# Two-layer attention and retention trunk: background steps of the first group named round by round, and another order of the first supertile's list

## The chip, the core and the metric

The kernel runs on one core of a Trainium2 chip. The core has a matrix engine (TensorE, PE in the profile; its weight loads are PEld), a vector engine (VectorE, DVE), an activation engine (ScalarE, ACT), a general engine (GpSimd, POOL) and a queue that issues transfers (SyncE, SP). Each works through its own instructions in order and waits at the head of its queue for what the next instruction needs from another engine or a transfer. The metric is the device time of one execution in microseconds, the median over several runs.

## What is computed

Two layers over 2048 tokens of width 1024, float32 in and out, and a final RMS norm. The reference, cut to what matters:

```python
def hybrid_layer(x, norm_gain, w_in, w_out, rel_bias, cos, sin):
    hn = rms_norm(x, norm_gain)
    proj = hn @ w_in                       # 1024 x 4096
    aq, ak, av, ag, rq, rk, rv, rg = jnp.split(proj, cuts, axis=-1)
    ya = chunked_rel_attention(aq, ak, av, rel_bias)      # 8 heads x 64, own chunk + 8 before
    yr = chunkwise_retention(rq, rk, rv, cos, sin)        # 4 heads x 128, recurrent state
    y = jnp.concatenate([ya * silu(ag), yr * silu(rg)], axis=-1)
    return x + y @ w_out

def reference(x, positions, norm_gain, w_in, w_out, rel_bias, final_gain):
    cos, sin = rotary_tables(positions, RET_HEAD_DIM)
    for layer in range(DEPTH):
        x = hybrid_layer(x, norm_gain[layer], w_in[layer], w_out[layer], rel_bias[layer], cos, sin)
    return rms_norm(x, final_gain)
```

## The kernel before

**Precision.** Every large product is made of float16 halves: an operand is scaled by a power of two, its upper half is a float16 copy (ACT, the "hi" steps) and the remainder is a second float16 (DVE, the "lo" steps); three products of halves are added in PSUM. So normalised tokens are `hTh` and `hTl`, weights `wh` and `wl`.

**Tiling.** The tokens are 16 tiles of 128, four to a supertile of 512 (n = 0 to 3). The heads of a layer are four groups (s = 0 to 3) of two attention heads and one retention head. For each layer, group and supertile there is `dense_T` (L652), four outputs of 24 matmuls (q, k, rotary q and k, heads on the partitions), then `dense_V` (L784), four token tiles of 24 matmuls (v, retention v, gates), then `attention` (L823) with `retention` (L913). The attention of a supertile runs while the next supertile's dense work runs.

**Rounds.** `run` (L1222) walks through the dense generator. Eight dense matmuls are a round; `dense_T` and `dense_V` have 12 each. In each round, `run` first lets the dense generator issue its matmuls and, after 24, their eviction from PSUM; then `tick` issues small steps that were put off by a number of rounds with `later`; then one step of attention; then `pull` takes steps from background generators in `bg`, as many as needed to be done in time. All engines but SP take this written order. SP takes it up to the end of the first supertile (`sp_order`); after that the transfers are ordered by the framework, but for those under `in_turn`.

Attention issues the scores of a unit (token tile and head) every third round: matmuls (L845, L846), the bias and maximum on DVE (L849, L851), the exponential on ACT (L852), a float16 copy (L854), its remainder on POOL (L855), and a transposing transfer (L857). Retention's products (L902) need a masked score (DVE L921), its upper half (ACT L906) and the remainder (DVE L910), one round apart, and the same for the state `sh`.

**Before the first round.** The first supertile is ordered by hand in one list of step names, `do(...)` (L1433). Steps of token tile t: `xsq` square and sum (ACT), `xrs` root (a small DVE step L217 and a power on POOL L219), `xmul` product with the root and the gain (DVE), `xtr` transposes on PE, `xhi`, `xlo`, `xdma` transposing transfers on SP. Steps of weight section j, W for `dense_T` and V for `dense_V`: `sq` (ACT), `lp` a cast of the sum (DVE L1315), `sc` a sum over partitions on PE (L1321) and the scale (DVE L1328 to L1332), `hi`, `lo`. `g` computes the gain's scale, `t` and `u` are steps of the rotary tables 0, and 1 and 2, `r` reverses the relative bias, `bs` and `bt` spread it, `d` is a step of the first `dense_T`, `Tu` and `Vu` are small scale factors.

**Background in the first group (s = 0).** During `dense_V` of supertile 0 a generator of 12 rounds (L1438) finishes token tiles 4 to 7. During supertiles 1 and 2, `norms_from_input` (L1236) normalises token tiles 8 to 11 and 12 to 15, one after the other on a plan of 21 rounds, and the rotary tables run beside them; the sine is taken on ACT (L118, L119). During supertile 3, `prep_T` (L393) prepares the weights of `dense_T` of the next group; with its `dense_V` begins `prep_V` (L442), the weights of that group's `dense_V`. How many steps fall into one round is worked out by `run`.

**Shared buffers that the prediction names.** PSUM has two buffers for dense outputs, so an output waits until the one two before it was evicted by ACT and DVE (L677 and L680 for q, `qq`; L694 and L697 for k, `kk`; L805 to L815 for dense_V). The buffer of `qq` is also that of rk's `raw` in the first supertile, and `kk`, `swp` share one. `swp` receives the swapped halves by transfer (L715, L716), POOL rotates (L719 to L721), ACT and DVE split (L724, L727).

Of the kernel before, what the change touches and what calls it, by code (L numbers as in the profile page):

```python
# [8 lines left out]
F16 = mybir.dt.float16  # L9
# [4 lines left out]
ALU = mybir.AluOpType  # L14
# [4 lines left out]
P = 128  # L19
# [8 lines left out]
def hybrid_trunk(ctx: ExitStack, tc: tile.TileContext, x, pos, gain, gcol, w_in, w_out, rel, fgain,  # L28
# [364 lines left out]
    def prep_T(l, s, g, halves=False, w=None):  # L393
        w = w or Sections(l, s, g, halves)
        if (l, s) == (0, 1):
            w.load(0)
            w.load(1)
            for j in range(4):
                for _ in range((2, 2, 0, 1)[j]):
                    yield  # L400
                w.square(j)
                if j in (0, 2):
                    w.load((j + 4) // 2)
                yield
                if j:
                    w.scale(j - 1)
                    yield from w.split(j - 1)
            yield
            w.scale(3)
            yield from w.split(3)  # L410
            return
# [242 lines left out]
    def dense_T(l, s, n, g, st):  # L654
# [4 lines left out]
        def tab_load():  # L659
            while n not in tab_done:  # L660
                pull(1)
            in_turn(sp.dma_start(st.tabc, tab_d[n][0]))
            in_turn(sp.dma_start(st.tabs, tab_d[n][1]))
# [103 lines left out]
        for j in range(2 if first else 0, 4):  # L767
            if j == 2 and not first:
                tab_load()
            if first:  # L770
                ps = psR.tile([P, 512], F32, tag="small", name=f"dT{nm}_{j}")
            else:
                ps = psD.tile([P, 512], F32, tag="dense", name=f"dT{nm}_{j}")
            while g.tdone <= j:
                pull(1)
            m = 0
            for kt, (w_, h_) in in_order(j == 0, ((g.h, hh), (g.l, hh), (g.h, hl))):
                pe.matmul(ps, w_[:, j, kt, :], h_[:, kt, :], start=(m == 0), stop=(m == 23))  # L778
                m += 1
                if m in (8, 16) or (m == 24 and first):  # L780
                    yield
            evacuate(j, ps)
            yield

    def dense_V(l, s, n, g, st):
# [4 lines left out]
        st.rv, st.g = [], []  # L790
        while g.vdone < 4:
            pull(1)
        for a in range(4):
# [441 lines left out]

    def norms_from_input(ts, spaces, rows, tab):  # L1236

        def load(k):
            u = us[k]
# [4 lines left out]
        def sq(k):  # L1244
            u = us[k]
# [3 lines left out]
        def root(k):  # L1249
            us[k].rs = rms_of(us[k].ss, gains[0].m, gains[0].e, us[k].nm)  # L1250

        def mul(k):
            u = us[k]
            dve.scalar_tensor_tensor(out=u.x, in0=u.x, scalar=u.rs[:, 0:1], in1=gains[0].b, op0=ALU.mult, op1=ALU.mult)

        def hi(k):
            us[k].rows = rows[k % 2]
            rows_hi(us[k].rows, us[k].x)

        def lo(k):  # L1260
            rows_lo(us[k].rows, us[k].x)

        def dma(k):
            transpose_rows(us[k].rows, *us[k].h)

        us = []
        for t in ts:
            u = St()
            u.t, u.nm = t, f"n0_{t}"
            us.append(u)  # L1270
        plan = {0: [lambda: load(0)]}
        add = lambda r, fn, k: plan.setdefault(r, []).append(lambda: fn(k))
        for k in range(4):
            if k:
                add(4 * k - 4, load, k)
            for i, fn in enumerate((sq, root, mul, hi, lo, dma)):
                add(3 + 4 * k + i, fn, k)
        for r in range(21):
            for fn in plan.get(r, ()):
                fn()  # L1280
            next(tab, None)
            yield
        for _ in tab:
            yield

# [141 lines left out]

    def rounds(lists):
        for names in lists:
            do(names)  # L1430
            yield

    do("xsq0 g g xrs0 g Wsq0 Wlp0 Wsc0 xmul0 xtr0 Whi0 xsq1 xhi0 xrs1 xlo0 xmul1 Wlo0 xsq2 d t Wsq1 xrs2 xtr1 t xhi1 Wlp1 xmul2 "  # L1433
# [3 lines left out]
    g00.vdone = 4  # L1437
    push(rounds(["xhi4 xrs5 xrs6", "xlo4 xmul5 xrs7", "xdma4 xhi5 xmul6 bt", "xlo5 xhi6", "xdma5 xlo6 xmul7", "xdma6 xhi7",  # L1438
                 "xlo7", "xdma7 bt", "x8 u", "u x8 bt", "u u x8", "u u x8 bt"]), 12)
    att = [None]  # L1440
    for l in range(DEPTH):
        gO = [Grp(), Grp()]
        go = Grp()
        for s in range(NSW):
            g = grp(l, s)
            for n in range(NS):
# [12 lines left out]
                if (l, s) == (0, 0) and 0 < n < NS - 1:  # L1459
                    if n == 1:  # L1460
                        push(t1, TAB_STEPS - 7)
                    pairs = [xs0[0], w4.tile([P, D], F32, tag="w4", name="rows8") if n == 1 else xs0[1]]
                    pairs = [(w_[:, 0:D], w_[:, D:2 * D]) for w_ in (r_.bitcast(F16) for r_ in pairs)]
                    push(norms_from_input(range(4 * n + 4, 4 * n + 8), late[0:4] if n == 1 else None, pairs,
                                          iter(()) if n == 1 else tables((3,), [xs0[3][:, i * 256:(i + 1) * 256] for i in range(4)])), 21)
                if (l, s, n) == (0, 1, 1):
                    for l_ in range(1, DEPTH):
# [3 lines left out]
                        later(18, lambda gr=gr: next(gr))  # L1471
                if n == (NS - 1 if (l, s) == (0, 0) else 1):
                    if s + 1 < NSW:
                        push(prep_T(l, s + 1, grp(l, s + 1)), 25 if (l, s) != (0, 0) else 19)
                    else:
# [9 lines left out]
                if not first:  # L1485
                    run(dT, att, 12 if last else 10 if n == 0 else 18 if (l, s, n) == (0, 0, NS - 1) else 22 if (l, s) == (0, 0) else 24)
                if n == NS - 1:
                    if s + 1 < NSW:
# [94 lines left out]
```

## Time and profile before

| | us |
|---|---|
| median of 3 runs | 2059.97 (2055.54 to 2060.03) |
| the profiled execution | 2058.52 |
| its span, first to last instruction | 2056.7 |
| PE busy in the span | 1996.4 |
| DVE busy | 1239.1 |
| ACT busy | 1134.8 |
| POOL busy | 685.7 |

How to read it: an engine's busy time is the time in which it executes instructions, not waits. The mean clock granted to PE over the span is 0.993 of full speed. Matmuls are pipelined, so the duration of one (some 0.38 us for 512 columns) is longer than the distance between two starts. A row of waits names the waiting engine, its tile and line, the instruction that ended the wait, the total in us, how often, and the longest.

### The profile page before, as it was taken

To read this page: it belongs to the slowest core of one execution; us is meant where nothing else is said; L and a number is where in the kernel's file an instruction comes from. 1 tells how busy PE (TensorE), PEld (TensorE's weight loads), DVE (VectorE), ACT (ScalarE), POOL (GpSimd) and SP (SyncE) were. 2 spreads that over 40 slices of the span, in tenths; PEclk is the share of its full clock that TensorE was granted. 3 is DMA by queue.
4 is the path that set the end of the run, shared out by engine and by line. 5 is a ranking of instruction groups with operands and counts; after the bars stand their busy time and mean duration, and the time that the engine had idled before them with its cause. 6 is when DMAs were issued, how large, how long until landed. Compare 5 with 4: busy or idle time off the path is not lost. (4 is left out here: it accounts for less than half of the span.)

```text
span 2056.7 us, 36849 instructions
## 1 busy us (share of the span) xinstructions
PE 1996.4 (97%) x12918; PEld 1048.5 (51%) x12918; DVE 1239.1 (60%) x3676; ACT 1134.8 (55%) x2526; POOL 685.7 (33%) x701
## 2 busy tenths in 40 slices
PE   6998999999999999999999999999999999999998
PEld 4444554555555555554444555555555555555444
DVE  7676666566556655667553656565655566557543
ACT  7556665556565654655444546554656565455432
POOL 0243343444344433430003433443343434343100
PEclk9999999999999999999999999999999999999999
DMA  8677764557584754799874547454656765558874
GB/s 233 165 167 171 156 148 108 113 110 167 112 185 112 165 135 103 161 205 276 223 180 114 129 104 156 116 126 102 160 118 147 155 155 129 123 116 185 226 203 137
DMA packets 645690, 313.47 MB, mean 152 GB/s; under 512 B 459232, under 2 KB 602080, under 8 KB 645504
## 3 DMA queue, kind: packets, MB, share of 16 engines
q1 hardware_dynamic: 645504, 311.12, 64.8%
q8 instruction: 101, 1.65, 0.3%
q14 instruction: 85, 0.70, 0.1%
HBM read 123.26 MB, written 41.98 MB: 80 GB/s over the span
## 5 line engine op out<-in xcount | busy, mean ns | idle before, releaser
L855 POOL TENSOR_TENSOR pq<-sc,pq 128x640 f16<-128x640 f32 (+4 forms) x256 | 319.7, 1249 | 862.9 <-ACT pq L854 445.4
L852 ACT ACTIVATE sc<-sc,mq,cT 128x640 f32<-128x640 f32 (+4 forms) x256 | 218.4, 853 | 615.7 <-DVE mq L851 448.5
L797 PE MATMUL dV<-whV,hTh 128*128 128x512 f16 x1024 | 352.8, 380 | 4.8 <-DVE gt L815 4.6
L797 PE MATMUL dV<-whV,hTl 128*128 128x512 f16 x1024 | 352.8, 380 | 0.0
L797 PE MATMUL dV<-wlV,hTh 128*128 128x512 f16 x1024 | 352.5, 380 | 0.0
L778 PE MATMUL dT<-hTh,whT 128*128 128x512 f16 x1008 | 348.6, 381 | 3.7 <-DVE kk L697 1.3
L778 PE MATMUL dT<-hTl,whT 128*128 128x512 f16 x1008 | 347.2, 380 | 0.0
L778 PE MATMUL dT<-hTh,wlT 128*128 128x512 f16 x1008 | 347.2, 380 | 0.0
L797 PEld LDWEIGHTS <-hTh 128*128 128x128 f16 x2048 | 196.3, 98 | 221.4 <-DVE gt L815 7.0
L778 PEld LDWEIGHTS <-whT 128*128 128x128 f16 x2016 | 192.5, 98 | 209.9 <-issue 4.6
L849 DVE CUSTOM_DVE_ANT_0 sc<-S,bias 128x640 f32<-128x640 f32 (+4 forms) x256 | 188.4, 736 | 82.5 <-PE S L846 81.0
L1175 PE MATMUL dO<-whO,yhy 128*128 128x512 f16 x504 | 191.5, 380 | 1.5 <-DMA yhy<-hTh 1.5
L1175 PE MATMUL dO<-whO,yly 128*128 128x512 f16 x504 | 191.5, 380 | 0.5 <-DMA yly<-hTh 0.5
L1175 PE MATMUL dO<-wlO,yhy 128*128 128x512 f16 x504 | 191.7, 380 | 0.0
L854 ACT ACTIVATE pq<-sc 128x640 f16<-128x640 f32 (+4 forms) x256 | 171.5, 670 | 8.1
L1175 PEld LDWEIGHTS <-yhy 128*128 128x128 f16 x1008 | 98.3, 98 | 114.8 <-DMA yhy<-hTh 2.0
L797 PEld LDWEIGHTS <-hTl 128*128 128x128 f16 x1024 | 99.1, 98 | 111.9 <-issue 2.9
L778 PEld LDWEIGHTS <-wlT 128*128 128x128 f16 x1008 | 97.3, 98 | 114.7 <-issue 7.3
L845 PE MATMUL S<-k,q 128*128 128x128 f16 (+3 forms) x592 | 142.8, 268 | 0.0
L867 PE MATMUL o<-v,pT 128*128 128x129 f16 x1120 | 133.8, 222 | 5.4 <-DMA pT<-pq 5.4
L846 PE MATMUL S<-k,q 128*128 128x128 f16 (+3 forms) x592 | 129.7, 267 | 0.0
L868 PE MATMUL o<-v,pT 128*128 128x65 f16 x1120 | 126.8, 194 | 0.0
(359 smaller groups left out, 3246.1 us busy)
## 6 DMA issues: line engine op xcount, KB each, us to landing
q<-qq SPq DMA_DIRECT2D x128, 128.0 KB, 2.4
yyy<-y_d SPq DMA_DIRECT2D x32, 512.0 KB, 4.4
stT<-in_w_in_dram SPq DMA_DIRECT2D x27, 512.0 KB, 5.2
stV<-in_w_in_dram SPq DMA_DIRECT2D x26, 512.0 KB, 4.5
k<-kk SPq DMA_DIRECT2D x128, 64.0 KB, 2.0
swp<-rot SPq DMA_DIRECT2D x64, 128.0 KB, 3.1
tabc<-tab SPq DMA_DIRECT2D x32, 256.0 KB, 2.9
tabs<-tab SPq DMA_DIRECT2D x32, 256.0 KB, 3.1
```

What stands on the lines that cost most here:

```text
L778: pe.matmul(ps, w_[:, j, kt, :], h_[:, kt, :], start=(m == 0), stop=(m == 23))
L797: pe.matmul(ps, h_[:, kt, a * P:(a + 1) * P], w_[:, kt, :], start=(m == 0), stop=(m == 23))
L845: pe.matmul(o, st.q[:, hx, 0, cs], k_, start=True, stop=False)
L846: pe.matmul(o, st.q[:, hx, 1, cs], k_, start=False, stop=True)
L849: dve.tensor_tensor_reduce(out=v, in0=S[:, 0:w], in1=g.bias[hx][:, 640 - w:640], scale=1.0, scalar=-3.0e38, op0=ALU.add, op1=ALU.max, accu ...
L852: act.activation(v, v, AF.Exp, bias=m[:, 0:1], scale=g.c[:, 0:1])
L854: act.activation(pq[:, 0:w], v, AF.Copy)
L855: pool.tensor_tensor(pq[:, w:2 * w], v, pq[:, 0:w], op=ALU.subtract)
L867: pe.matmul(o[:, u.hx, 0:129], u.p[:, b, :], v_, start=(b == 0), stop=False)
L868: pe.matmul(o[:, u.hx, 0:65], u.p[:, u.nb + b, :], v_[:, 0:65], start=False, stop=(b == u.nb - 1))
L1175: pe.matmul(ps, h_[:, kt, :], w_[:, kt, :], start=(m == 0), stop=(m == 23))
```

## The change

The generators of the first group are replaced by named steps. `listed` has 96 entries, one for each round from `dense_V` of supertile 0 to the end of `dense_T` of the next group's supertile 0: rounds 0 to 11 are `dense_V` of supertile 0, 12 to 35 supertile 1, 36 to 59 supertile 2, 60 to 83 supertile 3, 84 to 95 that `dense_T`. An entry has two lists of names: the first is issued ahead of attention's step of the round, the second behind it. Later rounds have nothing listed, and `pull` works as before for the other groups.

```diff
@@ run
         for _ in gen:
             tick()
+            before, behind = next(listed, ("", ""))
+            do(before)
             if att[0] is not None and next(att[0], att) is att:
                 att[0] = None
             ring["att_done"] = att[0] is None
+            do(behind)
```

`norms_from_input` becomes `norm_steps`, which registers the same functions under names: `xin8` to `xin15` (the load; nothing is issued for 8 to 11, which `x8` loads), then `xsq`, `xrs`, `xmul`, `xhi`, `xlo`, `xdma`. `weight_steps` registers those of the next group's weights: `Tin`, `Tsq`, `Tsc`, `Thi`, `Tlo` for `dense_T` and `Uin`, `Usq`, `Usc`, `Uhi`, `Ulo`, `Uu` for `dense_V`, made from the same helpers as `prep_T` and `prep_V`; the special case for (0, 1) in `prep_T` goes.

```diff
+    def norm_steps(ts, spaces, rows):
...
+        for k, t in enumerate(ts):
+            u = St()
+            u.t, u.nm = t, f"n0_{t}"
+            for f, fn in (("in", load), ("sq", sq), ("rs", root), ("mul", mul), ("hi", hi), ("lo", lo), ("dma", dma)):
+                steps[f"x{f}{t}"] = lambda fn=fn, u=u, k=k: fn(u, k)
+
+    def weight_steps():
+
+        g = grp(0, 1)
+        w = Sections(0, 1, g)
...
+        def vsq(j):
+            m[j] = sumsq(sts[j], f"{nm}{j}", g.vh[:, :, j * P:(j + 1) * P])
+            if j == 3:
+                dve.tensor_tensor(m[2], m[2], m[3], op=ALU.add)
+            if j != 2:
+                m[j] = lowp(m[min(j, 2)], f"{nm}{j}")
+
+        def vsc(j):
+            sv, iv[j] = norm_scale(allsum(m[j if j < 2 else 3], f"{nm}{j}"), f"{nm}{j}", gains[0].i)
+            for i in ((j,) if j < 2 else (2, 3)):
+                vcv[i] = convert(sts[i], g.vh[:, :, i * P:(i + 1) * P], g.vl[:, :, i * P:(i + 1) * P], sv)
...
+        for j in range(4):
+            for f, fn in (("in", w.load), ("sq", w.square), ("sc", w.scale), ("hi", thi), ("lo", lambda j: drain(cv[j]))):
+                steps[f"T{f}{j}"] = lambda fn=fn, j=j: fn(j)
+            for f, fn in (("in", vload), ("sq", vsq), ("sc", vsc), ("hi", lambda j: next(vcv[j])), ("lo", vlo)):
+                steps[f"U{f}{j}"] = lambda fn=fn, j=j: fn(j)
+        steps["Uu"] = units
```

The lists themselves (`v` is a step of rotary table 3):

```diff
-    do("xsq0 g g xrs0 g Wsq0 Wlp0 Wsc0 xmul0 xtr0 Whi0 xsq1 xhi0 xrs1 xlo0 xmul1 Wlo0 xsq2 d t Wsq1 xrs2 xtr1 t xhi1 Wlp1 xmul2 "
-       "Wsc1 xsq3 Wsq2 xrs3 t xtr2 xlo1 xhi2 d Whi1 t xlo2 Wsq3 xmul3 d r Vsq0 Wlp2 Wlo1 t Wsc2 xtr3 Vsq1 r d xhi3 "
-       "t Vlp0 Whi2 Vsc0 t xlo3 Whi3 bs t d Vhi0 Wlo2 d Vhi1 Wlo3 t d d d Vlo0 t t Vsq2 d t Vlo1 t u Vsq3 t d Vlp2 t d t Tu Vsc2 t xsq4 "
-       "Vhi2 Vhi3 d d Vlo2 Vlo3 xsq5 d Vu d xsq6 xrs4 d Vu xmul4 xsq7 d")
+    do("xsq0 g g Wsq0 xrs0 Wlp0 xsq1 g Wsc0 t Whi0 xmul0 t xtr0 xrs1 Wlo0 xmul1 xsq2 xhi0 xrs2 Wsq1 xlo0 xtr1 xsq3 "
+       "Wlp1 xmul2 Wsc1 d xhi1 Whi1 xtr2 xrs3 xlo1 xhi2 t Wsq2 xlo2 Wsq3 xmul3 t Wlo1 d d Wlp2 Vsq1 r xtr3 t Vsq0 Wsc2 "
+       "d Vlp0 t xhi3 t Vsc0 Whi3 t xlo3 Vsq3 d Whi2 t r Vsq2 d Wlo2 t Vhi0 d d Wlo3 d bs Vlp2 d t Vlo0 d Vhi1 t xsq7 "
+       "t xsq4 d t Tu t xrs4 t t Vsc2 xmul4 xsq6 Vhi3 d Vhi2 u Vlo1 d Vlo2 d Vu xsq5 d Vlo3 Vu d d")
     g00.vdone = 4
-    push(rounds(["xhi4 xrs5 xrs6", "xlo4 xmul5 xrs7", "xdma4 xhi5 xmul6 bt", "xlo5 xhi6", "xdma5 xlo6 xmul7", "xdma6 xhi7",
-                 "xlo7", "xdma7 bt", "x8 u", "u x8 bt", "u u x8", "u u x8 bt"]), 12)
+    listed = iter([("bt xrs6 xhi4 xrs5", "xmul6 xlo4 xdma4"), ("xrs7 xmul5", ""), ("xhi5", "xmul7 xlo5"), ("", "xhi6 x8"),
+                   ("", "xdma5 u xlo6"), ("", "u xhi7"), ("xlo7 bt", ""), ("bt u", "u"), ("", ""), ("u u u", ""),
+                   ("", "xdma6 xdma7"), ("x8 u", "bt"), ("", "u x8"), ("u x8 xin11", ""), ("u", "u u u u"), ("", "u"),
+                   ("", "u"), ("", ""), ("", ""), ("xin9 xin8", ""), ("xsq8", "xrs8 xin10"), ("xsq9", "xmul8 xhi8 xrs9"),
+                   ("", "xmul9"), ("xhi9 xlo8", ""), ("xsq10", "xlo9"), ("xdma9", ""), ("xsq11 xdma8", "xrs10"),
+                   ("", "xrs11 xmul10"), ("xhi10", ""), ("", "xmul11 xlo10"), ("xhi11", "xlo11"), ("", "xdma10 xdma11"),
+                   ("", ""), ("", ""), ("", ""), ("", ""), ("xin12", ""), ("", "v"), ("xsq12", "xin13 v"), ("", "v"),
+                   ("xin14 v v", "xrs12 v"), ("xsq14 xmul12", ""), ("xhi12", "xlo12"), ("v v", "xsq13 xdma12"),
+                   ("v xrs13", "xrs14"), ("", "v"), ("xmul13", "xin15"), ("xhi13", ""), ("v", "v xlo13"),
+                   ("xmul14 v", ""), ("", "v xsq15"), ("xhi14 xrs15", "v"), ("xlo14 xdma13", "xmul15 xdma14"),
+                   ("", "v xhi15"), ("", ""), ("xlo15", ""), ("xdma15", ""), ("v", ""), ("v", ""), ("", ""),
+                   ("Tin0", "Tin1 Tsq1"), ("", ""), ("", "Tsq0"), ("", "Tin2"), ("", "Tsc1"), ("Tsc0 Tsq2", "Thi0"),
+                   ("", ""), ("Thi1 Tlo0", ""), ("", ""), ("", "Tsc2 Tlo1 Tin3"), ("", ""), ("Tsq3", ""),
+                   ("Thi2", "Tsc3"), ("", "Tlo2 Thi3 Tlo3"), ("", "Uin0"), ("Usq0", ""), ("", "Uin1"), ("", "Usc0 Uhi0"),
+                   ("", ""), ("Ulo0", ""), ("", ""), ("Usq1", ""), ("", ""), ("Usc1", "Uhi1"), ("", "Uin2 Ulo1"),
+                   ("", "Usq2"), ("Uin3", ""), ("Usq3", ""), ("", ""), ("", "Usc2 Uhi2"), ("", "Ulo2"), ("", ""),
+                   ("", "Uu Uhi3"), ("", ""), ("Ulo3", ""), ("", ""),])
```

Where the main loop pushed the generators for the first group it now registers steps:

```diff
-                    push(norms_from_input(range(4 * n + 4, 4 * n + 8), late[0:4] if n == 1 else None, pairs,
-                                          iter(()) if n == 1 else tables((3,), [xs0[3][:, i * 256:(i + 1) * 256] for i in range(4)])), 21)
+                    norm_steps(range(4 * n + 4, 4 * n + 8), late[0:4] if n == 1 else None, pairs)
+                    if n == 2:
+                        t3 = tables((3,), [xs0[3][:, i * 256:(i + 1) * 256] for i in range(4)])
+                        steps["v"] = lambda: go_on(t3)
...
-                if n == (NS - 1 if (l, s) == (0, 0) else 1):
+                if (l, s, n) == (0, 0, NS - 1):
+                    weight_steps()
+                elif n == 1 and (l, s) != (0, 0):
```

More of the change, by code (lines that the diff above doesn't have):

```diff
@@ L394, in prep_T @@
         w = w or Sections(l, s, g, halves)
[L395 to L411, printed above, removed]
         w.load(0)
@@ L1234, in run, with load @@
             left -= 1
-    def norms_from_input(ts, spaces, rows, tab):
-        def load(k):
-            u = us[k]
+    def norm_steps(ts, spaces, rows):
+        def load(u, k):
             u.x = spaces[k] if spaces else w4.tile([P, D], F32, tag="w4", name=f"xin{u.t}")
@@ L1254, in mul, with hi @@
+        def mul(u, k):
             dve.scalar_tensor_tensor(out=u.x, in0=u.x, scalar=u.rs[:, 0:1], in1=gains[0].b, op0=ALU.mult, op1=ALU.mult)
[L1256 to L1267, printed above, removed]
+        def hi(u, k):
+            u.rows = rows[k % 2]
+            rows_hi(u.rows, u.x)
@@ L1268, in norms_from_input, with lo, dma @@
+        def lo(u, k):
+            rows_lo(u.rows, u.x)
+        def dma(u, k):
+            transpose_rows(u.rows, *u.h)
+        for k, t in enumerate(ts):
             u = St()
             u.t, u.nm = t, f"n0_{t}"
[L1270 to L1277, printed above, removed]
```

49 lines of the change are left out of this document (28 added, 21 removed).

## The prediction

> **What bounds the kernel now.** I read the page's span and busy times first, then the waits of TensorE (PE), then the busy time of each engine by supertile, and last the queues of the other engines around the waits.
>
> ```profile
> span 2056.7 us, 36849 instructions
> PE 1996.4 (97%) x12918; PEld 1048.5 (51%) x12918; DVE 1239.1 (60%) x3676; ACT 1134.8 (55%) x2526; POOL 685.7 (33%) x701
> ```
>
> PE is the bound: 60.3 us of the span are without a matmul. No matmul is added or removed by the change, so it can win only PE's pauses and the time in which PE ran at a lower clock. Where those lie is seen by cutting the trace at the first dense matmul of each supertile. The columns are start:end, length, then busy us of PE, PEld, DVE, ACT and POOL, the granted clock, the DMA share and GB/s.
>
> ```profile
> 0.00:50.37 50.37, 33.31 (x298) 24.22 (x299) 35.82 (x105) 36.06 (x68) 4.88 (x18) 0.93 0.81 234
> 50.37:71.33 20.96, 20.89 (x97) 9.29 (x96) 17.12 (x29) 13.19 (x27) 6.51 (x8) 1.00 0.81 155
> ...
> 71.33:130.77 59.44, 51.51 (x278) 24.66 (x277) 42.30 (x96) 32.45 (x73) 23.48 (x26) 0.94 0.70 171
> 130.77:191.83 61.06, 54.30 (x363) 28.77 (x361) 43.73 (x116) 37.08 (x78) 24.30 (x23) 0.97 0.82 173
> 191.83:248.72 56.89, 54.14 (x369) 29.10 (x370) 34.94 (x118) 36.10 (x80) 20.97 (x19) 0.97 0.69 150
> 248.72:304.27 55.55, 52.57 (x366) 28.18 (x364) 33.26 (x111) 35.45 (x83) 21.53 (x23) 1.00 0.71 158
> ...
> 353.95:405.78 51.83, 51.83 (x363) 28.03 (x361) 31.74 (x99) 28.16 (x67) 21.43 (x20) 1.00 0.51 113
> 405.78:457.85 52.07, 52.07 (x370) 28.35 (x367) 31.26 (x92) 27.74 (x63) 20.14 (x19) 1.00 0.53 112
> 457.85:509.71 51.86, 51.86 (x366) 28.08 (x364) 32.88 (x105) 33.05 (x80) 21.55 (x23) 1.00 0.74 167
> 509.71:557.88 48.17, 48.17 (x305) 24.73 (x303) 26.40 (x103) 27.47 (x71) 17.67 (x19) 1.00 0.50 111
> ```
>
> The last four rows are supertiles 2 and 3 of the second group and 0 and 1 of the third, where PE never pauses. They do the same matmuls as the four rows above them, in another order of the supertiles. So the excess of the first group is read directly: supertile 1, 59.44 - 48.17 = 11.3 us; supertile 2, 61.06 - 51.83 = 9.2; supertile 3, 56.89 - 52.07 = 4.8; supertile 0 of the second group, during whose first half the last listed steps run, 55.55 - 51.86 = 3.7. Together **29.0 us** in the rounds that the lists govern. Part of it is clock:
>
> ```profile
> 42.08:45.49 3.41, 3.41 (x10) 1.22 (x9) 0.97 (x8) 3.31 (x10) 0.00 (x0) 0.50 0.40 94
> 106.93:113.76 6.83, 5.96 (x24) 2.82 (x24) 5.06 (x13) 2.47 (x8) 4.21 (x6) 0.50 0.61 129
> 182.02:185.44 3.42, 3.42 (x20) 1.93 (x18) 1.71 (x6) 1.75 (x3) 0.02 (x1) 0.50 0.43 102
> 192.26:195.68 3.42, 3.42 (x18) 1.76 (x17) 1.26 (x5) 1.89 (x6) 1.40 (x1) 0.50 0.98 213
> ```
>
> Half clock for 3.41 us costs 1.7 us of PE's work. In the 29.0 us there are four such pieces (106.93 has two), 6.8 us; they follow PE's pauses. The rest are these pauses of PE from 50 to 304 us (last number: the longest) and one before 50 us:
>
> ```profile
> PE msV L334 <- DVE ya L881: 4.4, 3, 2.0
> PE r L902 <- DVE dT L910: 4.2, 6, 1.5
> PE dV L797 <- DVE gt L815: 3.3, 1, 3.3
> PE r L902 <- DVE sh L910: 2.4, 2, 2.0
> PE r L902 <- ACT dT L906: 1.4, 1, 1.4
> PE dT L778 <- DVE kk L697: 1.3, 1, 1.3
> PE dT L778 <- DMA hTh<-xa: 1.2, 1, 1.2
> PE dT L778 <- DVE qq L680: 1.2, 1, 1.2
> ...
> PE ms L1321 <- DVE mbV L1315: 2.5, 1, 2.5
> ```
>
> Nearly all wait for DVE, which was busy for only 42.30 of 59.44 us in supertile 1. DVE is late because it is itself held at the head of its queue by a background step, with attention's small steps behind it (DVE's waits from 71 to 280 us):
>
> ```profile
> DVE v L811 <- ACT rv L807: 10.1, 7, 5.1
> DVE mbT L327 <- ACT whT L320: 7.9, 4, 3.1
> ...
> DVE ssn L217 <- ACT hTh L212: 6.0, 4, 3.7
> DVE mbV L327 <- ACT whV L320: 5.6, 2, 2.8
> ...
> DVE xin L1254 <- POOL rsn L219: 2.0, 1, 2.0
> ```
>
> A square stands on ACT behind the exponentials of the same round, and the DVE step that needs the square stands in front of L910's remainder, for which PE waits.
>
> **The change part by part.** Matmuls, vector work and DMAs stay the same in number; the steps move. All figures are against the profiled execution's 2058.52 us (span 2056.7 plus 1.8 around it); the median shown, 2059.97, is 1.45 above that.
>
> Part 1, the first list (to 50.37 us). The step Vlp2 (DVE) now stands four d steps ahead of Vsc2 (PE), where it had one. The 2.5 us wait for mbV goes, and with it the half clock from 42.08: 2.5 + 1.7 = 4.2 us. Against it, the third g now stands behind Wlp0, which waits for W0's square. That g filled DVE's time from
>
> ```profile
> 6.97 0.16 DVE L336 TENSOR_SCALAR m2h<-msh 128x1 f32<-128x1 f32 x1 [0.20 <-PE msh L334]
> ...
> 8.25 0.15 DVE L196 SCALAR_TENSOR_TENSOR ge<-gi 128x1 f32<-128x1 f32 x1
> ```
>
> to 8.40, 1.43 us, while DVE waited for W0; now it delays Wsc0, xmul0 and the first transposes by as much. DVE is busy for 35.82 of these 50.37 us, so another 1 us may stick to xmul4, which now comes ahead of Vlo2 and Vlo3 (they have two more rounds, since dV's third term comes last). Bounds: +4.2 and, if both delays land on PE and the wait only moves, -2.5. I take a gain of **1.5 us**.
>
> Part 2, rounds 0 to 35. The copies that swap rk's halves stood on SP behind the transposes of token tiles 6 and 7:
>
> ```profile
> 68.87 1.28 SPq L244 DMA_TRANSPOSE hTl<-hTl  x1
> 70.25 0.54 SPq L715 DMA_DIRECT2D swp<-raw  x1
> ...
> 81.96 0.69 DVE L727 TENSOR_TENSOR rot<-raw,rot 128x512 f16<-128x512 f32 x1 [1.34 <-POOL pq L855]
> ```
>
> rk's remainder (L727) therefore came at 81.96, and PE waited for it and for qq, whose buffer it frees. With xdma6 and xdma7 in round 10 the swap (round 8) goes first; the waits for qq (1.2) and rot go. What it costs: four transposes at 1.28 are 5.1 us of SP, and rounds 10 and 11 give 3.5 us (20.96 / 12 each), so up to 1.6 us of wait in round 12 if SP reaches them only then; between 0 and that I take 1. The sines of tables 1 and 2 move from about round 16 to behind round 14, ahead of k's eviction in round 17: the kk wait (1.3) goes. The norms of tiles 8 to 11 have the square ahead of attention and the root behind it or two rounds later (xsq10 in 24, xrs10 in 26), and no product or remainder stands in rounds 25 and 26, where sh and dT were late and the 6.83 us of half clock followed. At most the whole 11.3 us goes; at least nothing.
>
> Part 3, rounds 36 to 59. The 3.3 us wait for gt is a table switch:
>
> ```profile
> 174.94 1.28 ACT L118 ACT_TABLE_LOAD   x1
> ...
> 178.24 1.28 ACT L806 ACT_TABLE_LOAD   x1
> ...
> 180.30 0.29 DVE L811 SCALAR_TENSOR_TENSOR v<-dV,v 128x128 f16<-128x128 f32 x1 [5.07 <-ACT rv L807]
> ```
>
> The sine stood ahead of one eviction of dV (L805 to L808). Now v16 stands behind round 53, whose dense part issues that eviction, and the next is three rounds on: two loads of 1.28 fit. The transposes of tile 15 move up to round 56, four rounds ahead of their use, so the 1.2 us wait for hTh<-xa goes. At most 9.2 us; xmul12 one round after xrs12 and xsq14 one round after xin14 can bring the 2.0 us wait of L1254 back, or hold ACT while a load lands.
>
> Part 4, rounds 60 to 95. The squares Usq0, Usq1 and Usq3 stand ahead of attention's exponentials, and their sums two rounds later: the msV waits (4.4) go. Tsq1 and Usq2 stand behind attention as before. At most 4.8 + 3.7.
>
> How much of the 29.0 goes? At the lengths of the quiet supertiles DVE would be busy 42.30 / 48.17 = 88% in supertile 1 and 43.73 / 51.83 = 84% in supertile 2; the nearest row is 50.37 to 71.33, which ran at 17.12 / 20.96 = 82% with PE 20.89 of 20.96 busy, though without attention. So DVE's work fits, with little slack. I leave 4 us in supertile 1, 3 in 2, 2 in 3 and 1.5 in the last, 10.5 in all, and so a gain of 7.3 + 6.2 + 2.8 + 2.2 = **18.5 us**. With part 1: 20.0, so 2058.5 - 20.0 = 2038.5, say **2039 us**.
>
> On the clock, the half-rate rows last 3.41 us or twice that, and the one at 42.08 followed a wait of 2.5 us. The Trainium skill (TensorE: Matmul & The Clock Gate, HAM oscillation) wants no idle gap over some 3.4 us. By it the small waits I leave would cost only themselves, and the estimate stands. By this trace's 2.5 us wait each of three could bring 1.7 us more, some 5 us.
>
> **The rivals.** (a) *Nearly all pauses go*: 4 us stay of the 29.0 and the first list wins 3.5: 2058.5 - 28.5 = 2030. For it: the quiet rows show such rounds without any pause. Against: DVE at 88%. (b) *The waits move to other steps*: the clock pieces stay and half of the other 22.2 us is given back at the new places: 2058.5 - 11.1 + 2 = 2050, with a loss of 2 in the first list. For it: xmul9 directly behind xrs9, four table steps in round 14. (c) *No change*: supertiles 1 and 2 keep their length, because DVE was the bound there all along, and 3 and 4 win 2: 2057. Against: DVE idles 17 us in each of the two. (d) *Slower*: the chain square, root, power, product holds DVE at every one of the eight tiles, because the power stands on POOL behind attention's pq. Price by the longest rows: 3.7 (ssn for ACT) + 2.0 (L1254 for POOL) = 5.7 each, 46 us for eight. DVE's work of 42.30 + 43.73 plus 46 is 132 us against 120.5 now: 11.5 us slower, **2070**. It decides from a mean hold of (120.5 - 86.0) / 8 = 4.3 us per tile; now ssn held it four times for 6.0 together. That the lists don't do what they say is not a case: every listed step is issued from them.
>
> **How the numbers follow.** The forecast 0.50, (a) 0.13, (b) 0.17, (c) 0.08, (d) 0.12. The measurement tells about 0.3% (6 us) from no change. Faster: the forecast, (a) and (b), 0.80; same: (c), 0.08; slower: (d), 0.12. The forecast's own range is 2032 to 2047 (5 to 17 us left of the 29.0, first list between -2.5 and +4.2). The range of 8 in 10 reaches over (a) and (b): 2028 to 2055.
>
> **What would show it.** In the changed profile: supertiles 1 and 2 of the first group near 52 and 55 us long, no half clock between 100 and 200 us; no wait of PE for gt, qq or kk; msV waits under 1 us together; rk's swap ahead of the transposes of tile 7; the first dV matmul near 49 us. I am wrong if the first dV matmul comes after 52 us, if PE waits in round 12 for hTh by more than 3 us, or if DVE's waits for ssn and rsn grow over 8 us together.

## The result and the profile after

| | us |
|---|---|
| changed kernel, median of 4 runs | 2043.49 (2038.22 to 2046.1) |
| kernel before on the same chip, median of 4 runs | 2058.02 (2055.54 to 2060.03) |
| ratio, with its 95% interval | 0.9927 [0.9902, 0.9951] |
| the changed kernel's profiled execution | 2046.1 |

The kernel is faster by 0.7%. Profiled execution against profiled execution it wins 2058.52 - 2046.1 = 12.4 us, where the forecast's sum was 20.0. The changed kernel's profiled execution is the slowest of its four; by the medians the gain is 14.5 us. The page of the changed kernel:

```profile
span 2044.0 us, 36842 instructions
PE 1992.2 (97%) x12918; PEld 1047.1 (51%) x12918; DVE 1249.5 (61%) x3676; ACT 1136.1 (56%) x2526; POOL 694.1 (34%) x701
```

Its trace cut at the same places as before, the first dense matmul of each stage, with the columns of the first such table: the first list, `dense_V` of supertile 0, supertiles 1, 2 and 3, and supertile 0 of the next group. The last three rows are all the pieces of half clock up to 420 us.

```profile
0.00:44.51 44.51, 30.65 (x298) 23.59 (x299) 34.83 (x103) 35.44 (x66) 4.75 (x18) 1.00 0.88 253
44.51:69.34 24.83, 20.88 (x98) 9.34 (x97) 23.06 (x40) 14.70 (x33) 12.24 (x11) 0.97 0.89 196
69.34:125.46 56.12, 52.19 (x278) 24.91 (x279) 35.94 (x91) 33.49 (x72) 22.34 (x25) 0.92 0.68 166
125.46:180.94 55.48, 52.87 (x364) 27.85 (x362) 47.05 (x104) 35.35 (x74) 27.43 (x22) 1.00 0.80 165
180.94:240.04 59.10, 54.10 (x370) 29.01 (x371) 38.83 (x127) 37.32 (x82) 21.11 (x19) 0.97 0.76 167
240.04:292.07 52.03, 52.03 (x365) 28.06 (x363) 34.76 (x109) 35.74 (x83) 22.51 (x24) 1.00 0.83 168
67.96:74.78 6.82, 5.44 (x15) 2.17 (x16) 2.79 (x8) 2.24 (x5) 2.68 (x4) 0.50 0.90 281
119.16:122.57 3.41, 3.41 (x13) 1.49 (x14) 3.34 (x14) 1.76 (x7) 0.55 (x1) 0.50 0.99 195
194.25:197.66 3.41, 3.34 (x18) 1.92 (x19) 1.20 (x5) 0.06 (x1) 0.00 (x0) 0.50 1.06 243
```

Set beside the rows of before, stage by stage: 

| stage | before | after | change | forecast |
|---|---|---|---|---|
| first list | 50.37 | 44.51 | -5.9 | -1.5 |
| `dense_V` of supertile 0 | 20.96 | 24.83 | +3.9 | 0 to +1 |
| supertile 1 | 59.44 | 56.12 | -3.3 | -7.3 |
| supertile 2 | 61.06 | 55.48 | -5.6 | -6.2 |
| supertile 3 | 56.89 | 59.10 | +2.2 | -2.8 |
| supertile 0, next group | 55.55 | 52.03 | -3.5 | -2.2 |

The sum of the changes is -12.2. So the gain came, but not where it was put: the first list won four times its term, the next 12 rounds gave two thirds of that back, and supertile 3 became longer. The waits of PE from 46 to 300 us tell what PE waits for now:

```profile
PE o L853 <- DMA pT<-pq: 10.0, 7, 2.7
PE dT L763 <- DVE xa L94: 3.9, 1, 3.9
PE r L888 <- DVE dT L896: 1.1, 2, 0.9
PE r L888 <- DVE sh L896: 0.3, 1, 0.3
```

The waits for gt, qq, kk, mbV and ya are gone, and those for DVE's remainders fell to 1.4 us. What took their place is on SP: 10.0 us for attention's transposing transfers (pT), for which PE had waited 0.4 us before, and 3.9 us in front of round 12. The releaser of the second row is misnamed: L94 is a step of the rotary tables, which no matmul of `dense_T` reads. What round 12 does read are the transposes of token tiles 6 and 7. DVE had finished their rows early (the remainders of the two tiles):

```profile
55.36 2.29 DVE L286 TENSOR_TENSOR hTl<-hTl,hTl 128x1024 f16<-128x1024 f32 x1
...
60.39 1.21 DVE L286 TENSOR_TENSOR hTl<-hTl,hTl 128x1024 f16<-128x1024 f32 x1
```

so tile 6 was ready at 57.65 us and tile 7 at 61.60. The order on SP (start, time to issue) shows where they stood:

```profile
58.14 2.35 SPq L244 DMA_TRANSPOSE hTl<-hTh  x1
60.54 0.58 SPq L593 DMA_DIRECT2D bias<-toep  x1
61.63 0.49 SPq L699 DMA_DIRECT2D swp<-raw  x1
...
62.85 1.30 SPq L243 DMA_TRANSPOSE hTh<-hTl  x1
...
67.23 1.29 SPq L244 DMA_TRANSPOSE hTl<-hTl  x1
```

Tile 6's first transpose went out 5.2 us after its row was complete, behind tile 5's last transpose, the bias and rk's swap; tile 7's last was out at 68.5, and PE went on at 69.34.

The pT waits have two forms. In the transfers of pT from 105 to 125 us one landed in 5.3 us, where the middle one took 2.9; ahead of it SP had issued two loads of token tiles of 512 KB each:

```profile
DMA to landing us min/median/max: 2.6/2.9/5.3
```
```profile
112.77 0.90 SPq L1230 DMA_DIRECT2D xin<-in_x_dram  x2
113.78 1.23 SPq L843 DMA_TRANSPOSE pT<-pq  x1
```

PE waited 2.6 us for it, and half clock followed at 119.16. Neither the loads nor the long landing is new. In the kernel before the same two loads stood straight ahead of the same pT, the sixth of that supertile, which landed in 5.00 us, and PE did not wait for it:

```profile
117.18 2.12 SPq L1242 DMA_DIRECT2D xin<-in_x_dram  x2
119.41 1.23 SPq L857 DMA_TRANSPOSE pT<-pq  x1
```

What changed is who comes when. Counted from the first matmul of the supertile, PE now stands at that matmul 47.1 us in, where it came 54.8 in; POOL has the row ready at 39.1 instead of 45.2; SP issues the transpose at 44.4 instead of 48.1. PE and the row gained 6 to 8 us and SP, which works through the transfers in front, less than 4. So, as far as the two traces show, a late transfer that PE's waits for DVE had hidden came to light when these went.

At 182 us another pT stood on SP behind stores of a rotary table, and the next was itself long in issue behind two loads, that of the next group's weights (L305) and that of a gain (L163):

```profile
181.42 0.59 SPq L128 DMA_DIRECT2D tab<-xb  x1
182.12 1.33 SPq L843 DMA_TRANSPOSE pT<-pq  x1
...
186.04 0.44 SPq L305 DMA_DIRECT2D stT<-in_w_in_dram  x1
186.53 0.58 SPq L163 DMA_DIRECT2D gb<-in_gain_dram  x1
187.21 2.96 SPq L843 DMA_TRANSPOSE pT<-pq  x1
```

PE paused 2.45 and 2.88 us there; with the half clock at 194.25 that is 7.0 us, as much as supertile 3 is longer than its quiet row (59.10 - 52.07).

### The profile page after: what moved, and what is told of

It is laid out like the page before. It is cut to its first block, busy times and chain, and to the rows that moved or that the text cites. A ratio compares the mean times of both kernels' runs of the same rounds, so it can differ in the third digit from the quotient of the medians.

```text
span 2044.0 us, 36842 instructions
## 1 busy us (share of the span) xinstructions
PE 1992.2 (97%) x12918; PEld 1047.1 (51%) x12918; DVE 1249.5 (61%) x3676; ACT 1136.1 (56%) x2526; POOL 694.1 (34%) x701
## 5 line engine op out<-in xcount | busy, mean ns | idle before, releaser
L853 PE MATMUL o<-v,pT 128*128 128x129 f16 x1120 | 133.1, 222 | 14.7 <-DMA pT<-pq 14.6
L853 PEld LDWEIGHTS <-pT 128*128 128x128 f16 x1120 | 103.5, 98 | 50.7 <-DMA pT<-pq 22.6
```

Of the source, the lines that this page charges most:

```text
L853: pe.matmul(o[:, u.hx, 0:129], u.p[:, b, :], v_, start=(b == 0), stop=False)
```

## The experiments

Unless another base is named, a kernel is the changed one with the edit shown. "Stage" is a row of the stage table; a pause is the distance between two matmuls' starts less the time the first one takes at full pace (0.22 us for 512 columns). A profile is one execution: behind the lists, where all kernels are written alike, the fourteen traces take 1748.5 to 1753.8 us. So a row of a stage is a better witness than 2 or 3 us between two medians; of the intervals below only those of `e1` and `f4` lie clear of the changed kernel's.

**Each half alone.** `e1_first_list` is the kernel before with only the new `do(...)` list. 

> Kernel before with only the first list of the change. Theory (the parts add up by stage): the first dV matmul comes at 44.5 us as in the changed kernel (before 50.4), supertiles 1 to 3 of the first group and supertile 0 of the second keep the lengths of the kernel before (59.4, 61.1, 56.9, 55.6), so 2058 - 4 to 6 = 2052 to 2054. Rival (tiles 4 to 7 set the pace): the first dV matmul comes early but the first matmul of supertile 1 still at 70 to 71 us, since DVE and SP prepare tiles 4 to 7 no sooner; then nothing is left of the gain, 2056 to 2058.

Measured 2052.6 us, ratio 0.9978 [0.9964, 0.9992], as the theory had it; its third stage:

```profile
65.46:126.72 61.26, 52.01 (x279) 24.80 (x278) 43.67 (x101) 34.03 (x76) 23.87 (x27) 0.94 0.70 169
```

The first list alone brings supertile 1 forward by 71.33 - 65.46 = 5.9 us, and supertile 1 itself takes 1.8 more. `e2_round_lists` is the changed kernel with the old first list.

> Changed kernel with the first list of the kernel before; the lists by rounds stay. Theory: first dV matmul at 50.4 us, and since supertile 0 then has 5.9 us more, the wait of 3.9 us in round 12 is gone; supertiles 1, 2, 3 and the next 0 as in the changed kernel (56.1 less 3 for the half clock in it, 55.5, 59.1, 52.0): 2044 to 2047, so the first list is worth little by itself. Rival (the first list carries a third or more of the gain): 2049 to 2052.

Measured 2043.8 us, 0.9931 [0.9917, 0.9946], the same as the whole change. A wait of 1.8 us in round 12 stayed, which the expectation had gone. So by the medians the parts do not add: alone they win 0.2% and 0.7%, together 0.7%. Where the first list's 6.5 us go (44.51 against 51.05) the traces show in part. At the first matmul of supertile 1 the changed kernel is still 4.9 us ahead (69.34 against 74.25), at the end of the lists 1.3 (292.07 against 293.40). Between the two it has 12.3 us of half clock and `e2` 3.4, a difference of 4.4 us of work. That covers the 3.6 us that are lost there, so most of the lead goes into half clock behind pauses and not in front of round 12. Whether it goes so in every execution was not tested.

**Round 12: SP's order or late rows?** `e3_turns_earlier` moves the transposes alone.

```diff
-    ("", "u xhi7"), ("xlo7 bt", ""), ... ("", "xdma6 xdma7")
+    ("xdma6", "u xhi7"), ("xlo7 xdma7 bt", ""), ... ("", "")
```

> Changed kernel with the transposes of tile 6 in round 5 and of tile 7 in round 6, ahead of the second bias tile and of rk's swap on SP. Theory (SP's order makes the wait in round 12): the rows of tile 6 are ready at 57.7 us and those of tile 7 at 61.6, SP has them out 2.3 us sooner, and the wait of 3.9 us before the first matmul of supertile 1 falls under 2; the half clock behind it goes too, 1.5 to 3.4; rk's swap comes 5 us later and stays ahead of its use: 2.5 to 5 us faster than the changed kernel. Rival (DVE is late, as the row that names DVE xa says): the wait stays at 3.5 to 4.5 and the time is the changed kernel's.

Measured 2045.38 us, 0.9939 [0.9922, 0.9956]. The pause in front of round 12 fell from 4.1 to 2.0 us, and `dense_V` of supertile 0 to 22.7: the order makes the wait. But the swap now went out at 68.32 instead of 61.63 us, and the waits that the lists had removed were back:

```profile
PE dT L763 <- DVE rv L799: 1.8, 1, 1.8
...
PE dT L763 <- DVE qq L664: 1.2, 1, 1.2
```

Supertile 1 took 60.4. It is a trade between two transfers on one queue, and the 2.5 to 5 us that were expected did not come.

`f1_round12` also takes out what competes: the first load of token tiles 8 to 11 (x8; the expectation calls it a load of weights, but it reads x) goes from round 3 to 11, the second bias from 7 and 11 to 10 and 13, the transposes to rounds 7 and 9.

```diff
-    ("", "xhi6 x8"), ... ("bt u", "u"), ("", ""), ("u u u", ""), ("", "xdma6 xdma7"), ("x8 u", "bt"), ("", "u x8"), ("u x8 xin11", "")
+    ("", "xhi6"), ... ("xdma6 u", "u"), ("", ""), ("xdma7 u u u", ""), ("", "bt"), ("x8 u", "x8"), ("", "u x8"), ("u x8 xin11", "bt")
```

> The changed kernel with four steps of rounds 3 to 13 in other rounds: the first load of the next group's weights (x8) goes from round 3 to 11, the transposes of token tile 6 from round 10 to 7, those of tile 7 from round 10 to 9 (behind rk's swap of round 8), the second spreading of the bias from rounds 7 and 11 to 10 and 13. Theory (the 4.1 us wait of PE ahead of round 12 is SP's order: the tiles' rows are ready at 57.7 and 61.6 us but stand behind bias and swap, and their transfers compete with the 1 MB of weights): the gap in front of supertile 1 falls from 4.1 to under 2 us, the 6.8 us of half clock at 68 us go, and dense_V of supertile 0 takes 21 to 22.5 us instead of 24.8; supertile 1 stays at 55 to 57 us, since the swap keeps its place; in all 2.5 to 4 us less, a median of 2039 to 2042. Rival 1 (the trade that the earlier turn of the transposes showed): qq's wait comes back, supertile 1 grows by 3 us or more and the sum of the two stages stays at 80 to 82. Rival 2 (the rows themselves are late, because DVE is full): the gap stays above 3.5 us.

Measured 2040.91 us, 0.9914 [0.9894, 0.9934]. SP:

```profile
59.20 1.29 SPq L243 DMA_TRANSPOSE hTh<-hTl  x1
...
62.34 0.53 SPq L699 DMA_DIRECT2D swp<-raw  x1
```

Tile 6 goes ahead of the swap now, and the swap keeps its place. The wait is 1.7 us, the half clock at 68 us is gone, `dense_V` takes 22.5 and supertile 1 53.7: 76.2 for the two instead of 80.9, and no wait for qq. The theory held; both rivals fell. Four steps moved at once, so which of them did most is open.

**pT beside the loads.** `e4_loads_in_turn` fixes the loads of token tiles 12 to 15 to their written places; the framework had moved two of them up.

```diff
-    sp.dma_start(u.x, x[u.t * P:(u.t + 1) * P, :])
+    in_turn(sp.dma_start(u.x, x[u.t * P:(u.t + 1) * P, :]))
```

> Changed kernel with the loads of token tiles 12 to 15 kept at their written place on SP; two of them stood ahead of a transpose of pT at 112.8 us, and now stand ahead of a later one. Theory (a transpose issued behind 1 MB of loads lands in 5.3 us in place of 2.9): the PE wait of 2.7 us at 116 us and the half clock from 119.2 go, 3 to 4.4 us, and the transpose that now follows the two loads, the first of supertile 2, lands in about 5 us; whether PE waits for that one decides how much is kept. Rival (that transpose is late because DVE and POOL are): the wait at 116 us stays.

Measured 2045.41 us, 0.9941 [0.9926, 0.9956]. The wait at 116 us and its half clock went, and supertile 1 took 51.9 as expected, but supertile 2 took 59.9 instead of 55.5. The waits of ACT there say why:

```profile
ACT hTh L212 <- DMA xin<-in_x_dram: 10.3, 2, 6.7
```

In the lists xsq12 stands two rounds behind its load and xsq14 one, and ACT's queue stood at them for 3.5 and 6.7 us, with the exponentials behind. `f3_loads_spaced` has the same `in_turn`, with xin12, 13 and 14 in rounds 29, 32 and 35 instead of 36, 38 and 40.

> The changed kernel with the loads of token tiles 12 to 15 fixed to written places on SP and apart from each other (rounds 29, 32, 35 and 46; the lists had them in 36, 38, 40 and 46, and the framework moved two of them up together to 112.8 us). Theory (the 2.7 us wait at 116 us with its half clock is a transpose of pT that lands in 5.3 instead of 2.6 to 2.9 us beside two loads of 512 KB; where the loads come as late as in the lists, ACT's squares wait for them and supertile 2 pays): supertile 1 at 52 to 53.5 us without the half clock at 119, supertile 2 at 54.5 to 56.5; a median of 2037 to 2041. Rival (supertile 1 has a fixed slack: whichever transfers go near round 33, a pT falls behind one): the wait is found again at another round from 29 to 35, supertile 1 stays at 55 to 57; median 2042 to 2046.

Measured 2036.54 us, 0.9899 [0.9879, 0.9919]; supertiles 1 and 2:

```profile
69.59:121.72 52.13, 50.78 (x278) 24.43 (x279) 34.98 (x85) 31.73 (x68) 20.63 (x24) 0.94 0.67 159
121.72:176.88 55.16, 52.58 (x363) 27.70 (x361) 48.12 (x113) 37.01 (x77) 28.77 (x24) 1.00 0.88 188
```

Both as expected: transfers of pT and loads apart from each other, and early enough, cost nothing in supertile 2.

**pT behind the stores.** `f2_stores_and_gain` fixes the gain's load (L163) to its written place with `in_turn`, and divides the table's stores between rounds 59 and 62.

```diff
     for hf in range(2):
         store(0, ns[0], hf)
+        if ns == (3,) and hf == 0:
+            yield
```

> The changed kernel with the eight stores of table 3 divided between two rounds (59 and 62, instead of all at once) and its two steps before them at rounds 55 and 59, and with the load of the next layer's gain fixed to its place in SP's written order. Theory (the two waits of PE in supertile 3, 2.45 us at 182 and 2.88 us at 191, are attention's transposes of pT that stand on SP behind eight stores, and that land late behind the loads of stT and the gain): both waits fall under 1 us, the half clock at 194 us goes, supertile 3 takes 52.5 to 55.5 us instead of 59.1; a median of 2037 to 2041. Rival (pT is late since DVE, POOL or ACT make pq late in these rounds, in which the squares and loads of the next group's weights begin): supertile 3 stays at 57.5 to 60 us, with the same length of waits under another name; median 2042 to 2046.

Measured 2040.55 us, 0.9915 [0.9897, 0.9932]. The second pause fell from 2.88 to 1.54 us and the half clock at 194 went; supertile 3 took 56.1, between the bounds of theory and rival and nearer to the theory's. The first pause stayed at 2.4: the stores did not move on SP (175.23 to 185.07 us; in the changed kernel 175.59 to 185.36), since the framework orders them, wherever the list names them. `f4_all` has the edits of f1, f2 and f3.

> The three edits of this batch together on the changed kernel. Theory (the three places are separate: round 12, pT beside the loads, pT behind the stores): their gains add, 3 + 4 + 5 us, a median of 2030 to 2035, and no half clock behind the first dV matmul up to 300 us. Rival (each transfer that is moved meets the next one; DMA queues are the shared limit): under 4 us in all, 2040 to 2045.

Measured **2033.09 us, 0.9879 [0.9861, 0.9897]**, the fastest kernel of the study and faster than the changed kernel's interval. The theory held: 10.4 us by the medians, where the three alone won 2.6, 2.9 and 7.0. (The profiled execution, 2029.68, is the fastest of its four.) The stages after the first list, and the longest waits of PE from 46 to 300 us:

```profile
44.55:67.00 22.45, 20.88 (x98) 9.34 (x97) 20.72 (x36) 14.69 (x33) 9.93 (x9) 1.00 0.87 178
67.00:117.08 50.08, 48.28 (x278) 23.49 (x279) 36.89 (x88) 31.80 (x68) 23.34 (x26) 1.00 0.76 183
117.08:172.06 54.98, 52.53 (x364) 27.87 (x362) 48.02 (x113) 37.12 (x77) 27.72 (x24) 1.00 0.85 188
172.06:227.32 55.26, 52.50 (x373) 28.23 (x371) 38.59 (x125) 37.22 (x81) 21.99 (x19) 1.00 0.78 165
```
```profile
PE o L855 <- DMA pT<-pq: 4.7, 4, 1.5
PE dT L765 <- DMA hTh<-hTl: 1.6, 1, 1.6
```

The granted clock is 1.00 in every stage. DVE has the work it had (1247.5 us against 1249.5), so these waits were not DVE's fullness. `g5_stores_in_turn` adds `in_turn` to the eight stores.

> The kernel with the three edits together, and the eight stores of table 3 fixed to their written places on SP (the split between rounds 59 and 62 had not moved one of them: the framework issued all eight from 165.9 to 174.9 us, with a transpose of pT among them, as before). Theory (the wait for pT at 173.6 us, 1.5 us, is SP's order): that wait goes, supertile 3 takes 53.3 to 54.5 us instead of 55.3, a median of 2030 to 2033 against 2033 for the three edits. Rival (the pT lands when it does because its row is ready late or the transfers compete): wait and stage stay as they are.

Measured 2035.93 us, 0.9899 [0.9884, 0.9915]: the rival held. The stores went behind, and the pause was 2.5 us all the same, since the pT then followed two transposes of token tile 15 and a load of weights:

```profile
166.64 2.26 SPq L246 DMA_TRANSPOSE hTh<-xa  x1
169.00 1.56 SPq L247 DMA_TRANSPOSE hTl<-xa  x1
...
171.28 3.20 SPq L846 DMA_TRANSPOSE pT<-pq  x1
```

Moving those transposes wasn't tried.

**The removed waits, put back one at a time.** `m1_sine_ahead` names the sine one round earlier, so that two table loads stand in front of round 53's eviction again.

```diff
-    ("xlo14 xdma13", "xmul15 xdma14"), ("", "v xhi15")
+    ("xlo14 xdma13", "v xmul15 xdma14"), ("", "xhi15")
```

> The changed kernel with one step moved: the sine of rotary table 3 stands in round 52 behind attention, one round ahead of round 53's eviction of dV on ACT, instead of behind round 53. Theory (part 3 of the prediction: the 3.3 us wait of PE for gt was ACT's two table loads, one in front of the sine and one behind it, in front of that eviction): a wait of PE at L783 for gt of 2.5 to 3.5 us is back near 170 us, and supertile 2 takes 57.5 to 61 us instead of 55.5 (more than 1.7 of it half clock). Rival (the wait went because DVE and ACT have fewer steps in front of that eviction, and the place of the sine is free): no wait for gt over 1 us, supertile 2 at 54.5 to 56.5.

Measured 2050.86 us in one run. ACT has the loads where they were expected, at 169.09 and 171.37, but PE waits only 0.9 us for gt, and supertile 2 takes 55.4:

```profile
169.09 1.28 ACT L118 ACT_TABLE_LOAD   x1
...
171.37 1.28 ACT L792 ACT_TABLE_LOAD   x1
```
```profile
PE o L853 <- DMA pT<-pq: 10.6, 4, 6.4
...
PE dV L783 <- DVE gt L801: 0.9, 1, 0.9
```

So the rival's bounds were met: by itself the switch costs some 1 us there. The eviction of gt came 3.56 us later than in the changed kernel (172.67 against 169.11), and 2.7 of that was slack. In the kernel before more stood in front of the same eviction: the exponential had come 2.70 us late, and then a square:

```profile
172.19 0.92 ACT L852 ACTIVATE sc<-sc,mq,cT 128x640 f32<-128x640 f32 x1 [2.70 <-DVE mq L851]
...
173.78 1.04 ACT L212 ACTIVATE hTh<-xin 128x1024 f16<-128x1024 f32 x1
```

That these two had taken the slack there, so that the switch cost 3.3 us, is read from the trace; no run put them back.

What made this kernel slower neither theory had: a wait of 6.4 us for a pT in supertile 3 (61.6 us), with 10.2 us of half clock from 185.17 on, 2.2 us into the pause. Its row was ready at 178.76 us instead of 178.24 (the end of POOL's step), which is little of it. But with the sine elsewhere the framework chose another order on SP, and the pT stood behind a transpose of tile 15 and loads of weights:

```profile
180.90 2.32 SPq L244 DMA_TRANSPOSE hTl<-xa  x1
183.26 0.58 SPq L305 DMA_DIRECT2D stT<-in_w_in_dram  x1
183.95 3.02 SPq L843 DMA_TRANSPOSE pT<-pq  x1
```

`m2_squares_behind` puts Usq0, Usq1 and Usq3 behind attention's step, in the same rounds.

> The changed kernel with Usq0, Usq1 and Usq3, the squares of the next group's weights, behind attention's step of their rounds instead of ahead of it. Theory (part 4: the msV waits, 4.4 us in three, were squares that stood on ACT behind the exponentials): at least two waits of PE for ya at the sum over partitions (L334) are back, 2.5 to 4.5 us together; supertile 3 grows by 1.5 to 2.5 us from 59.1, supertile 0 of the next group by 1.5 to 2.5 from 52.0. Rival (the sums stand two rounds behind the squares now, and that alone is enough): msV waits stay under 1 us together and both stages within 1 us.

Measured 2048.39 us in one run; supertile 3 took 61.6 (+2.5), the next stage 52.8 (+0.7), and the row of before is back nearly to the number (4.4 then):

```profile
PE msV L334 <- DVE mbV L327: 4.2, 3, 2.6
```

The theory held for the waits, but two of the three (3.4 us) fell in supertile 3, and the next stage's 0.7 lies within the rival's bounds. Supertile 3 grew by 2.5 although the half clock at 194 us (1.7 us of work) did not come in this execution.

**The third g.** `h1_third_g` puts it ahead of Wlp0 again.

```diff
-    "xsq0 g g Wsq0 xrs0 Wlp0 xsq1 g Wsc0 t
+    "xsq0 g g Wsq0 xrs0 g Wlp0 xsq1 Wsc0 t
```

> The changed kernel with the third g of the first list ahead of Wlp0 again. Theory (part 1 of the prediction: this g fills DVE's wait for W0's square; in the changed kernel it delays xmul0 from 10.09 to 11.06 us and with it the first transposes): xmul0 starts near 10.1 us, PE's wait ahead of the first transposes is 2.3 instead of 3.3 us, and the first dV matmul comes at 43.3 to 44.2 us instead of 44.5. Rival (the delay is absorbed before the first dV matmul, since DVE is busy for most of the 44 us): the first dV matmul stays at 44.3 to 45.3. In either case the median of the whole stays within 0.3% of 2043.5, because dense_V of supertile 0 ends with the 4.1 us wait in round 12, whose rows are not made sooner by a g.

Measured 2042.38 us, 0.9935 [0.9918, 0.9951]. xmul0 starts at 10.16 instead of 11.06, and PE's pause ahead of the first transposes is 2.3 instead of 3.3 us; the pause ahead of the second ones grew from 1.7 to 2.7, and the first dV matmul came at 45.1. The rival held: the delay is real and is used up one tile later. (The other kernels with the new list begin dV between 44.06 and 45.68 us, so a microsecond is not clear from one trace here.)

## Why the prediction was right, and where it was not

The forecast, 2039 us from 2028 to 2055, and its sign held at 2043.49, inside its own narrower range of 2032 to 2047 too; the sum behind it was right in its kind and off in most of its terms. That the number came so near is in part luck: in the profiled execution the first list won 4.4 us more than its term, and the rounds won 6.3 where the sum had 18.5.

- **PE's pauses and half clock are all there is to win: right.** PE stands at 98% in the fastest kernel, and the gains by stage show as fewer pauses or a clock back at 1.00.
- **Part 1, 1.5 us: the term was mis-sized.** The first list won 5.9. The wait for mbV (2.5) went as said; the sum had one piece of half clock (1.7) and overlooked that the stage held another (from 18.18 us); both are gone. But the clock is not what the list won: `e2`, with the old list, ran this stage at 1.00 and still began dV at 51.05 (ACT waited 1.6 us longer there for a load of weights). DVE idles 9.7 us in the stage instead of 14.6; which of its waits made the difference was not tested. Of the losses, the third g's 1.43 was 1.0 on xmul0 and nothing at the end.
- **Round 12, "between 0 and that I take 1": the step that failed.** It counted SP's time to issue (5.1 us against 3.5) but not what stands in front on SP, nor that the tables' steps moved into these rounds (and the last sum has no line for the 1 us): DVE is busy for 23.06 of 24.83 us, and the transfers' share is 0.89. The pause was 4.1 us, and 74.78 - 69.34 = 5.4 us of the half clock that followed lay in supertile 1, 2.7 us of work. The text's own sign of error, a wait for hTh over 3 us, came. `e3` and `f1` show that SP's order makes more than half of it; 1.7 to 2.0 us stayed.
- **Parts 2 to 4, the waits removed: right.** No wait for qq, kk or gt and none for msV is left, the swap went ahead of tile 7 (and of 6), and DVE waits 1.7 us for ssn, so (d) fell; `e3` and `m2` brought qq's and msV's waits back by undoing their cause. For gt the named cause, the sine, costs 0.9 us by itself (`m1`); the rest of the 3.3 needed the late exponential and the square in front, as the trace reads. For kk and for DVE's remainders (dT and sh: 6.6 us before, 1.4 now) no run put the cause back.
- **"I leave 4 us in supertile 1, 3 in 2, 2 in 3 and 1.5 in the last": the total was mis-sized.** Left are 56.12 - 48.17 = 8.0, 55.48 - 51.83 = 3.7, 59.10 - 52.07 = 7.0 and 52.03 - 51.86 = 0.2: 18.8 us instead of 10.5. (The quiet row of supertile 1 has 305 matmuls against 278, so they are not quite the same; `f4`, at full clock, has PE busy for 48.28 there.) The rest was reckoned from DVE's fullness (88%), as if DVE's work stayed in its stage; the lists move some 6 us of it into the 12 rounds ahead. DVE ended at 36 of 56 us in supertile 1, and the leftover was on SP and in its transfers, an engine to which the sum gave one line. This is rival (b) in its form, waits that move, and in size the result lies between the two: 2046.1 in the profiled execution, where the forecast gave 2038.5 and (b) 2049.4. But (b) had looked for them at xmul9 and the table steps, on DVE and ACT.
- **"No half clock between 100 and 200 us": wrong** (119.16 and 194.25), and each follows a pT wait.
- **The Trainium skill's rule** (TensorE: Matmul & The Clock Gate, HAM oscillation: no idle gap over some 3.4 us) was weighed as the milder case. The runs lie between it and the harder case, nearer the harder, as the last section shows.

## What to carry to other kernels

When steps of a queue are renamed by hand, follow the queue that nobody writes, here SP's: which transposes, stores and loads will stand in front of the transfer that PE waits for next, and which large load shares its time. A DMA that is not fixed in its place goes where the framework puts it, and a step moved on another engine can change that order; so fix the transfers around a tight one, and fix a load only where its first reader stands far enough behind. When waits for one engine go, look for transfers that these waits had hidden: what stood in front of pT in supertile 1 stood there before, and cost nothing. And halves need not add: the two here were worth 0.2% and 0.7%, and 0.7% together.

## What the runs showed of the hardware

- **Half clock after short waits.** Of the pauses of PE between 2.3 and 3.5 us from 15 to 300 us in all fourteen traces, 16 of 27 were followed, within 5 us of their start, by half clock (3.41 us, once 6.83); the seven of 3.9 us and more all were, by 3.41 to 10.24 us. Pauses of the same place and length went both ways (2.45 us at 115.9 in `m2` did, 2.76 us at 115.2 in `h1` didn't), so a run's clock loss behind such a pause is not settled by its length. Shorter pauses did it too: in `e4` 2.1 and 1.3 us close together, with half clock from 150.12. In `f4`, whose longest pause is 1.7 us, no such piece is left up to 300 us. Executions of one kernel differ by it: the four of the changed kernel span 2036.1 to 2044.0 us at mean clocks of 0.998 to 0.995, and span times clock is 2032 to 2035 in all four. So where a profile has half clock behind a short pause, another execution may not.
- **Transposing transfers beside loads.** The transfer of pT (both float16 halves of a unit, 128 x 256 to 128 x 1280) lands in 2.3 us when it is smallest and in 2.9 when it is largest, at the quickest. From 46 to 300 us it takes 2.3 to 7.1 in the changed kernel (the middle one 3.2) and 2.3 to 6.5 in the kernel before (3.1): 5.3 behind two loads of 512 KB, 5.2 to 5.5 in `m1` and 7.1 at 187.21 behind loads of weights or the gain. Its time to issue on SP grows as well there, from 1.2 or 1.3 to 3.0 and 3.2 us, but not behind the two loads (1.23). A long landing alone costs PE nothing, as the 0.4 us of the kernel before show.
